# A hybrid decoder block on one core: thirteen Strassen pairs of V blocks instead of ten, their weights on SyncE's queue, and two groups of transposes moved

## The chip, the cores and the metric

The kernel runs on one core of a Trainium2 chip. The metric is the device time of one execution in microseconds, as the median of several runs. Engines are named as the profile names them: PE is TensorE's matmul and PEld its weight load, DVE is VectorE, ACT is ScalarE, POOL is GpSimd, SP is SyncE, which here does nothing but issue DMAs.

## What is computed

A decoder layer over 256 tokens of width 1024, in float32: two attention branches merged by gates, then a product-key expert mixer (PEER), residuals, and a last RMS norm. The mixer is the part that counts. There are 128 x 128 experts, each with a row u and a row v of 1024. Each token picks 16 experts for each of 8 heads, and

```python
act = gelu(einsum('td,thkd->thk', xc, u))     # u = expert_u[idx]
w = g * act                                   # g: softmax over the 16 best scores
y = einsum('thk,thkd->td', w, expert_v[idx])
```

The kernel does this densely: it multiplies all 16384 experts' u with all tokens, applies the gelu, multiplies by a matrix of gates that is zero where an expert was not picked, and multiplies the result with all of v.

## The kernel before

Weights come as a list of `units` of 128 partitions by up to 1024 columns, in the order of use: projections, attention's up-projections, gates, branches, `w_out`, queries, 128 U blocks, 128 V blocks. `emit_dma` takes the next unit, gives it a `raw` tile (a ring of 4) and has SyncE load it. `emit_split` splits the next unit into `hi` (ScalarE, L138) and `lo` = raw - hi (VectorE, for some stages POOL, L142), each in a ring of 4 tiles; it sees to it that three units beyond it are on their way. `wget(i)` splits up to unit i + 2 and hands out unit i. A product of two float32 matrices is three matmuls: hi with hi, hi with lo, lo with hi. All engines run their own instructions in the order in which the program emits them, and wait for each other through semaphores.

**Early.** `chunk(c)` multiplies the normed input with chunk c of the input projection, 4 units of 12 matmuls; `between` holds functions called behind a unit. Chunk 0 gives the latents, normed by `latent_norm` during chunk 1 (queries); `quad_T` transposes them (6 PE transposes, L263) and splits them into `cTh`, `cTl` (L272, L273) for the up-projections. Chunk 2 gives the keys, chunk 3 the values. `qa_evac` applies the rotary tables on VectorE and POOL (L410 to L417); `qa_T(1, kaT)` transposes the keys (8 PE transposes, L501; two copies by ScalarE, L503). Attention's first scores (L576) read `kaT`.

**U blocks.** `u_block` (wide, L851 and L853) and at the end `u_narrow` (L836 to L838) multiply block j of u with all tokens, and ScalarE writes the gelu into `gm[:, j, :]`, a tile of 128 x 128 x 256. The gates of the first 128 tokens lie in DRAM (`gd`), scattered there by POOL; the second half of the gelu of the first `NS` = 124 blocks is kept in `gld`, since the second tokens' gates are in `gm` already.

**V blocks.** `reload(j)` loads block j's part of `gd` and `gld` into `rl`; `a_mult(j)` multiplies `gm[:, j]` by it (L1161); `a_split(j)` makes `ah` (ScalarE, L1166) and `al` (VectorE, L1167) out of it, ring of 6 tiles of 256 columns; `v_mm(j, t)` adds block j for 128 tokens t to 1024 columns of the result in PSUM (L1188, 6 matmuls of 512 columns for each t).

**Strassen pairs.** For j in `WJ` the blocks j and j + 1 are taken together as a 2 x 2 product, in Winograd's form with seven products for eight (`w_mm`, L1265): 21 matmuls in place of 24. `w_pieces(j)` is a generator that one iteration at a time loads both blocks once more by POOL's queue (L1208, into spent parts of `gm`), forms four sums of their halves (L1211) and splits them (L1214, L1217) into `wsum`. `z_sums` and `z_split` do the like for the activations (L1247 to L1250, L1166, L1167). Four of the products collect in PSUM tiles `wm` over all pairs; `w_out` adds them to the residual after the last pair. The order of the V stage is written out by hand in its loop:

```python
for j in range(P):
    side += [w_pieces(i) for i in WJ if j == i - 11]
    a_split(j + 1); a_mult(j + 2); reload(j + 4)
    if j + 2 in WJ:
        a_mult(j + 3); z_sums(j + 2)
    vv[j] = (*wget(U_V[j]), *av.pop(j))
    if j + 1 in WJ:
        a_split(j + 2); z_split(j + 1)
    for g in side: next(g, None)
    # w_mm(j - 1) behind a pair, else v_mm(j, t) for both t
```

Of the kernel before, what the change touches and what calls it, by code (L numbers as in the profile page):

```python
# [11 lines left out]
F32 = mybir.dt.float32  # L12
# [5 lines left out]
OP = mybir.AluOpType  # L18
# [16 lines left out]
NB = 2  # L35
NP = 10

WJ = range(18, 108 + 1, 10)

C_ID, C_FREQ, C_W = 0, 128, 176  # L40
B_ID, B_MASK, B_I16, B_IOTA, B_W = 0, 128, 384, 640, 1664
# [3 lines left out]
def block_kernel(ctx, tc, consts, constb, pos, x, g_mix, g_ffn, g_fin, w_in, g_q, w_qup, g_kv, w_kvup,  # L45
# [68 lines left out]
    raw, split = {}, {}  # L114
    state = {"dma": 0, "split": 0, "end": len(units)}

    def emit_dma():
        i = state["dma"]
        if i >= state["end"]:
            return  # L120
        ap, w = units[i]
        raw[i] = wp.tile([P, 1024], F32, name="raw")
        nc.sync.dma_start(raw[i][:, :w], ap)
        state["dma"] += 1

    def emit_split(later=None, parts=1):
# [130 lines left out]
    def quad_T(src, dh, dl, t, b0, nb=4, scale=None, ps_=trt, diag=None, later=None):  # L257

        tr = ps_()
        for b in range(nb):  # L260
            bs = slice(b * P, (b + 1) * P)
            if diag is None:
                PE.transpose(tr[:, bs], src[:, bs], ident)  # L263
            else:
                PE.matmul(tr[:, bs], src[:, bs], diag, start=True, stop=True)
        tv = tr[:, :nb * P].rearrange("p (b n) -> p b n", b=nb)
        dst = (slice(None), slice(b0, b0 + nb), slice(t * P, (t + 1) * P))
        if later is not None:
            S.activation(dh[dst], tv, AF.Copy)
            later.append(lambda: V.tensor_tensor(dl[dst], tv, dh[dst].bitcast(F32), op=OP.subtract))  # L270
        elif scale is None:
            S.activation(dh[dst], tv, AF.Copy)  # L272
            V.tensor_tensor(dl[dst], tv, dh[dst].bitcast(F32), op=OP.subtract)  # L273
        else:
            S.activation(dh[dst], tv, AF.Copy, scale=scale)
            V.scalar_tensor_tensor(dl[dst], tv, scale, dh[dst].bitcast(F32), op0=OP.mult, op1=OP.subtract)
# [227 lines left out]

    qps = chunk(1, (lambda: latent_norm(0), lambda: latent_norm(1)))
    qa_evac(qps, 0)
    for t in range(NT):
        quad_T(cn[t][:, 512:], cTh, cTl, t, 0, nb=3)
    kps = chunk(2, (token_numbers,))
    qa_evac(kps, 1)  # L510
    qa_T(0, qaT)

# [19 lines left out]
    for hf in range(2):  # L532
        for t in range(NT):
# [7 lines left out]
            V.tensor_copy(vb[t][:, hf * 256:(hf + 1) * 256].rearrange("p (h z) -> p h z", h=4), kv[:, :, 64:])  # L541
            if hf == 0:
                G.tensor_copy(kd[:, :, 64:], kpe[:, t:t + 1, :].to_broadcast([P, H, 32]))
    vps = chunk(3)
    qa_T(1, kaT)
    for t in range(NT):
        S.activation(va[t], vps[t], AF.Copy, scale=rs1[t])

# [267 lines left out]
    def gelu_in(j, so, keep=False):  # L816
        S.activation(gm[:, j, T0], so[:, T0], AF.Gelu)
        if keep:
            gl = vpool[0].tile([P, T], F32, name="gl", tag="rl", bufs=4)[:, :P]
# [22 lines left out]
    def u_narrow(j, keep=False):  # L842
        gelu_in(j, u_mm(j), keep)
# [302 lines left out]
    av, rl = {}, {}  # L1146
    gview = gd.rearrange("(j i t) o -> j i (t o)", j=P, i=P)

    def reload(j):
        if j < P:  # L1150
            rl[j] = vp.tile([P, T], F32, name="rl", tag="rl", bufs=4)
            i = nc.sync.dma_start(rl[j][:, T0], gview[j]).ins
            for m in ends:
                tc.add_manual_dep(i, m.name, SYNC, reason="gates of all heads")
            if j < NS:
                nc.sync.dma_start(rl[j][:, T1], gld[j])

    def a_mult(j):
        if j in rl:
            w = T if j < NS else P  # L1160
            V.tensor_tensor(gm[:, j, :w], gm[:, j, :w], rl.pop(j)[:, :w], op=OP.mult)  # L1161

    def split2(src, w=T, **kw):
        h = vp.tile([P, T], F32R, name="ah", **kw)
        l = vp.tile([P, T], F32R, name="al", **kw)
        S.activation(h[:, :w], src, AF.Copy)  # L1166
        V.tensor_tensor(l[:, :w], src, h[:, :w].bitcast(F32), op=OP.subtract)  # L1167
        return h, l

    def a_split(j):  # L1170
        if j < P and j not in av:
            w = P if j in WJ else T
            av[j] = split2(gm[:, j, :w], w, tag="s1", bufs=6)

    yo = [[acc(), acc()], [acc(), acc()]]

# [17 lines left out]
    def spent(k):  # L1194
        return gm[:, 4 * k:4 * k + 4, :].rearrange("p a b -> p (a b)")

    copies = [[gm[:, 10 * k + a:10 * k + a + 4, :].rearrange("p a b -> p (a b)") for a in (0, 4)] for k in range(2)]
    zs = gm[:, 8:10, :].rearrange("p a b -> p (a b)")
    wsum = [h2[:, 2 * k:2 * k + 2].rearrange("p a z n -> p (a z n)") for k in range(4)]
    wm = {}  # L1200
    C0, C1 = slice(0, 512), slice(512, 1024)

    def w_pieces(j):
        r0, r1 = copies[WJ.index(j) % 2]

        def load(c):
            for k, r in enumerate((r0, r1)):
                G.dma_start(r[:, c], exp_v[:, j + k, c])  # L1208

        def add(o, a, b):  # L1210
            V.tensor_tensor(o, a, b, op=OP.add)  # L1211

        def upper(k):
            S.activation(wsum[2 * k], (r0, r1)[k], AF.Copy)  # L1214

        def lower(k, c):
            V.tensor_tensor(wsum[2 * k + 1][:, c], (r0, r1)[k][:, c], wsum[2 * k][:, c].bitcast(F32), op=OP.subtract)  # L1217

        load(C1)
        yield  # L1220
        load(C0)
        yield
        yield
        add(r1[:, C1], r1[:, C1], r0[:, C1])
        yield
        add(r0[:, C1], r0[:, C1], r0[:, C0])
        yield
        add(r0[:, C0], r0[:, C0], r1[:, C1])
        yield
        add(r1[:, C0], r1[:, C0], r0[:, C0])  # L1230
        yield
        upper(0)
        lower(0, C1)
        yield
        lower(0, C0)
        yield
        upper(1)
        lower(1, C0)
        yield
        lower(1, C1)  # L1240

    zz = {}

    def z_sums(j):
        a11, a21, a12, a22 = gm[:, j, T0], gm[:, j, T1], gm[:, j + 1, T0], gm[:, j + 1, T1]
        z = [zs[:, P * k:P * k + P] for k in range(4)]
        V.tensor_tensor(z[0], a22, a21, op=OP.subtract)  # L1247
        V.tensor_tensor(z[1], z[0], a11, op=OP.add)
        V.tensor_tensor(z[2], a11, a21, op=OP.subtract)
        V.tensor_tensor(z[3], a12, z[1], op=OP.subtract)  # L1250

    def z_split(j):
        zz[j] = [split2(zs[:, T * k:T * k + T], tag="z", bufs=4) for k in (1, 0)]

    def w_mm(j):
        (h0, l0, ah0, al0), (h1, l1, ah1, al1) = vv.pop(j), vv.pop(j + 1)
        z34, z12 = zz.pop(j)
        if not wm:
            for k, f in enumerate((trt, trt, sct, sct)):
                wm[k] = f()  # L1260

        def mul(o, st, ts, mv, cs, own=True):
            n = 0
            for a, b in ((0, 0), (0, 1), (1, 0)):
                PE.matmul(o, st[a][:, ts], mv[b][:, cs], start=own and j == WJ[0] and n == 0,  # L1265
                          stop=own and j == WJ[-1] and n == 2)
                n += 1

        s0, s1 = wsum[:2], wsum[2:]
        mul(wm[0], (ah0, al0), T0, (h0, l0), C0)  # L1270
        mul(yo[0][0], (ah1, al1), T0, (h1, l1), C0, False)
        mul(yo[0][1], z34, T1, (h1, l1), C1, False)
        mul(wm[1], z12, T0, s0, C1)
        mul(wm[2], z12, T1, s0, C0)
        mul(yo[1][0], (ah1, al1), T1, s1, C0, False)
        mul(wm[3], z34, T0, s1, C1)

    def w_out():

# [200 lines left out]
```

## Time and profile before

| | |
|---|---|
| median of 3 runs | 978.64 us (977.89 to 979.82) |
| the profiled execution | 974.74 us, of which the span is 973.0 |
| TensorE busy | 959.3 us, mean granted clock 0.997 |
| VectorE, ScalarE, POOL busy | 781.7, 605.7, 386.9 us |
| DMA | 217.51 MB, 224 GB/s over the span |
| U blocks | from about 245 to 623 us |
| V blocks | from 623 to 960 us |

A busy share is an average over stages, and TensorE's matmuls overlap, so its 99% does not say that it runs at its peak. What a stage is worth is read from what TensorE waits for in it, and from how far the other engines are from filling the time.

### The profile page before, as it was taken

How to read it: one execution, taken by the hardware profiler on the slowest of the kernel's cores; microseconds unless marked ns; L12 is line 12 of the kernel's file. 1: busy time of each engine (PE TensorE's matmuls, PEld its weight loads, DVE VectorE, ACT ScalarE, POOL GpSimd, SP SyncE). 2: the span in 40 equal slices, each digit the busy share in tenths (PEclk: the TensorE clock that was granted, in tenths of full speed). 3: DMA queues.
4: the chain of work that ended last, by engine and by line, in shares of the span. 5: the costliest groups of instructions: out<-in, count | busy, mean ns of one | idle time of the engine just before them, and what ended most of it. 6: DMA issues, size and time to landing. Idle time of an engine off the chain costs nothing.

```text
span 973.0 us, 16538 instructions
## 1 busy us (share of the span) xinstructions
PE 959.3 (99%) x5246; PEld 829.9 (85%) x5247; DVE 781.7 (80%) x1816; ACT 605.7 (62%) x1230; POOL 386.9 (40%) x289
## 2 busy tenths in 40 slices
PE   9999999999999999999999999999999999999996
PEld 6878888899998888888888888888888888888885
DVE  6845347658988888888888888689999999999984
ACT  6544453543566668888788877656666566656653
POOL 7644451177726877877877800001000000000001
PEclk9999999999999999999999999999999999999998
DMA  7755468564568888888988866798888988887871
GB/s 260 265 181 155 152 192 255 177 217 162 179 197 230 208 215 198 197 197 205 204 198 197 197 200 204 227 321 303 276 273 271 285 277 281 282 269 245 274 250 67
DMA packets 127945, 217.51 MB, mean 224 GB/s; under 512 B 29121, under 2 KB 78161, under 8 KB 127730
## 3 DMA queue, kind: packets, MB, share of 16 engines
q1 hardware_dynamic: 103248, 196.52, 64.1%
q0 software_dynamic: 20096, 11.25, 9.3%
q10 hardware_dynamic: 4514, 8.68, 2.3%
q8 instruction: 42, 0.69, 0.3%
q14 instruction: 45, 0.37, 0.1%
HBM read 197.72 MB, written 18.68 MB: 222 GB/s over the span
## 4 chain that ended last, share of the span: by engine, by line
PE 93%; POOL 2%; DMA 1%; DVE 1%; ACT 1%; issue 1%; SPq 0%; POOLq 0%; DVEq 0%; ACTq 0%
PE acc L1188 30%; PE tr L851 11%; PE sc L851 11%; PE tr L853 6%; PE sc L853 5%; PE sc L889 5%; PE acc L318 3%; PE acc L316 3%; PE acc L319 3%; PE acc L1265 2%; PE acc L1113 2%; PE sc L1265 1%; PE tr L1265 1%; PE sc L838 1%; PE sc L837 1%; PE sc L836 1%
## 5 line engine op out<-in xcount | busy, mean ns | idle before, releaser
L142 DVE TENSOR_TENSOR lo<-raw,hi 128x1024 fp32r<-128x1024 f32 (+1 forms) x277 | 332.2, 1202 | 53.0 <-ACT hi L138 51.0
L138 ACT ACTIVATE hi<-raw 128x1024 fp32r<-128x1024 f32 (+1 forms) x327 | 334.8, 1029 | 11.4 <-PE acc L319 5.2
L996 POOL DMA_INDIRECT gd<-gate,addr x128 | 210.8, 1647 | 78.9 <-issue 57.0
L1166 ACT ACTIVATE ah<-gm 128x256 fp32r<-128x256 f32 (+1 forms) x148 | 58.6, 409 | 131.9 <-DVE lo L142 71.4
L142 POOL TENSOR_TENSOR lo<-raw,hi 128x1024 fp32r<-128x1024 f32 x46 | 109.6, 2388 | 66.9 <-ACT hi L138 65.0
L1188 PE MATMUL acc<-hi,al 128*128 128x512 f32 x429 | 132.4, 389 | 0.0
L1188 PE MATMUL acc<-lo,ah 128*128 128x512 f32 x429 | 132.3, 389 | 0.0
L1188 PE MATMUL acc<-hi,ah 128*128 128x512 f32 x429 | 132.3, 389 | 0.0
L1208 POOL DMA_DIRECT2D gm<-in_exp_v_dram x40 | 21.8, 550 | 275.3 <-DVE h L1217 104.5
L851 PE MATMUL tr<-h,hi 128*128 128x512 f32 x464 | 116.2, 392 | 0.0
L851 PE MATMUL sc<-h,hi 128*128 128x512 f32 x448 | 112.3, 392 | 0.0
L851 PEld LDWEIGHTS tr<-h,hi 128*128 128x128 f32 x464 | 83.4, 189 | 14.9
L1188 PEld LDWEIGHTS acc<-hi,al 128*128 128x128 f32 x429 | 80.5, 188 | 16.8
L1188 PEld LDWEIGHTS acc<-lo,ah 128*128 128x128 f32 x429 | 80.5, 188 | 16.6
L1188 PEld LDWEIGHTS acc<-hi,ah 128*128 128x128 f32 x429 | 80.5, 188 | 16.6
L851 PEld LDWEIGHTS sc<-h,hi 128*128 128x128 f32 x448 | 80.6, 189 | 14.4
L1167 DVE TENSOR_TENSOR al<-gm,ah 128x256 fp32r<-128x256 f32 (+1 forms) x148 | 59.1, 410 | 14.6 <-ACT ah L1166 14.6
L853 PEld LDWEIGHTS tr<-h,lo 128*128 128x128 f32 x464 | 63.3, 190 | 4.5
L853 PEld LDWEIGHTS sc<-h,lo 128*128 128x128 f32 x448 | 61.1, 190 | 4.4
L853 PE MATMUL tr<-h,lo 128*128 128x256 f32 x464 | 64.7, 282 | 0.0
L853 PE MATMUL sc<-h,lo 128*128 128x256 f32 x448 | 62.5, 282 | 0.0
L1161 DVE TENSOR_TENSOR gm<-gm,rl 128x256 f32<-128x256 f32 (+1 forms) x128 | 52.1, 414 | 3.8 <-DMA rl<-gld 3.8
(343 smaller groups left out, 1668.3 us busy)
## 6 DMA issues: line engine op xcount, KB each, us to landing
raw<-in_exp_u_dram SPq DMA_DIRECT2D x128, 512.0 KB, 4.0
raw<-in_exp_v_dram SPq DMA_DIRECT2D x118, 512.0 KB, 4.8
raw<-in_w_in_dram SPq DMA_DIRECT2D x28, 512.0 KB, 3.5
gm<-in_exp_v_dram POOLq DMA_DIRECT2D x40, 256.0 KB
gd<-zero ACTq DMA_DIRECT2D x8, 1024.0 KB
raw<-in_w_pq_dram SPq DMA_DIRECT2D x16, 512.0 KB, 4.6
rl<-gd SPq DMA_DIRECT2D x128, 64.0 KB, 4.5
gld<-gs SPq DMA_DIRECT2D x124, 64.0 KB, 3.3
```

Of the source, the lines that this page charges most:

```text
L138: S.activation(hi[:, ks], r[:, ks], AF.Copy)
L142: e.tensor_tensor(lo[:, :w], r[:, :w], hi[:, :w].bitcast(F32), op=OP.subtract)
L316: PE.matmul(o, th[:, db, sl], lo[:, ws], start=False, stop=db == nd - 1)
L851: PE.matmul(s, hi[:, b * P:(b + 1) * P], h2[:, b].rearrange("p z n -> p (z n)"), start=b == 0, stop=False)
L853: PE.matmul(s[:, :T], lo[:, b * P:(b + 1) * P], h2h[:, b, :], start=False, stop=b == ND - 1)
L889: PE.matmul(q[:, :T], w[:, b * P:(b + 1) * P], m[:, b, :], start=k == 0 and b == 0, stop=k == 2 and b == ND - 1)
L996: i = nc.gpsimd.indirect_dma_start(out=gd[:, :], out_offset=bass.IndirectOffsetOnAxis(ap=addr[g][:, c], axis=0), in_=gate[g][:, c], in_off ...
L1161: V.tensor_tensor(gm[:, j, :w], gm[:, j, :w], rl.pop(j)[:, :w], op=OP.mult)
L1166: S.activation(h[:, :w], src, AF.Copy)
L1167: V.tensor_tensor(l[:, :w], src, h[:, :w].bitcast(F32), op=OP.subtract)
L1188: PE.matmul(o, st[:, sl], mv[:, c:d], start=j == (0 if own is None else P - LAST) and mv is hi and st is ah, stop=j == last and st is al)
L1265: PE.matmul(o, st[a][:, ts], mv[b][:, cs], start=own and j == WJ[0] and n == 0, stop=own and j == WJ[-1] and n == 2)
```

## The change

`WJ` becomes `range(18, 115, 8)`: 13 pairs, 8 blocks apart, where there were 10 at a distance of 10. The pieces of a pair are loaded by SyncE in place of POOL, once, into two fixed tiles `r0`, `r1`, from which the split of the two blocks is made as well (`loaded`); the sums go to tiles `xs` of their own and are split in four halves of 512 columns. `reload`, `a_mult` and `a_split` work on two blocks at a time. The z's are made by three operations in place of four and split into the unused columns of the first block's own `hi` and `lo`. In the early part, the transposes of the latents go behind the first unit of chunk 2 (the token numbers behind the second), and those of the keys behind the second unit of chunk 3.

```diff
-WJ = range(18, 108 + 1, 10)
+WJ = range(18, 114 + 1, 8)
...
         ap, w = units[i]
-        raw[i] = wp.tile([P, 1024], F32, name="raw")
-        nc.sync.dma_start(raw[i][:, :w], ap)
+        if i in loaded:
+            raw[i] = loaded.pop(i)
+        else:
+            raw[i] = wp.tile([P, 1024], F32, name="raw")
+            nc.sync.dma_start(raw[i][:, :w], ap)
...
-    for t in range(NT):
-        quad_T(cn[t][:, 512:], cTh, cTl, t, 0, nb=3)
-    kps = chunk(2, (token_numbers,))
+    def latent_T():
+        for t in range(NT):
+            quad_T(cn[t][:, 512:], cTh, cTl, t, 0, nb=3)
+    kps = chunk(2, (latent_T, token_numbers))
...
-    vps = chunk(3)
-    qa_T(1, kaT)
+    vps = chunk(3, (lambda: None, lambda: qa_T(1, kaT)))
...
     def reload(j):
         if j < P:
-            rl[j] = vp.tile([P, T], F32, name="rl", tag="rl", bufs=4)
-            i = nc.sync.dma_start(rl[j][:, T0], gview[j]).ins
+            rl[j] = vp.tile([P, 2, T], F32, name="rl", tag="rl", bufs=3)
+            i = nc.sync.dma_start(rl[j][:, :, T0], gview[j:j + 2].rearrange("j i t -> i j t")).ins
...
-            V.tensor_tensor(gm[:, j, :w], gm[:, j, :w], rl.pop(j)[:, :w], op=OP.mult)
+            V.tensor_tensor(gm[:, j:j + 2, :w], gm[:, j:j + 2, :w], rl.pop(j)[:, :, :w], op=OP.mult)
...
+            h, l = [vp.tile([P, 2 * T], F32R, name=n, tag="s1", bufs=4) for n in ("ah", "al")]
+            split2(gm[:, j:j + 2, :].rearrange("p a b -> p (a b)"), h, l)
...
+    r0, r1 = spent(0), spent(1)
+    xs = [gm[:, 8 + 2 * k:10 + 2 * k, :].rearrange("p a b -> p (a b)") for k in range(4)]
+    zs = gm[:, 16:18, :].rearrange("p a b -> p (a b)")
...
             for k, r in enumerate((r0, r1)):
-                G.dma_start(r[:, c], exp_v[:, j + k, c])
+                nc.sync.dma_start(r[:, c], exp_v[:, j + k, c])
+                loaded[U_V[j + k]] = r
...
         load(C1)
         yield
         load(C0)
         yield
         yield
+        add(2, r1[:, C1], r0[:, C1])
+        yield
+        add(0, r0[:, C1], r0[:, C0])
+        upper(2)
+        yield
+        add(1, r0[:, C0], xs[2])
+        lower(2)
+        upper(0)
+        yield
+        add(3, r1[:, C0], xs[1])
+        yield
+        lower(0)
+        upper(1)
+        yield
+        lower(1)
+        upper(3)
+        yield
+        lower(3)
...
     def z_split(j):
-        zz[j] = [split2(zs[:, T * k:T * k + T], tag="z", bufs=4) for k in (1, 0)]
+        zz[j] = [t[:, C1] for t in split[U_V[j]]]
+        split2(zs, *zz[j])
...
-        mul(wm[1], z12, T0, s0, C1)
-        mul(wm[2], z12, T1, s0, C0)
-        mul(yo[1][0], (ah1, al1), T1, s1, C0, False)
-        mul(wm[3], z34, T0, s1, C1)
+        mul(wm[1], z12, T0, s0, C0)
+        mul(wm[3], z34, T0, s1, C0)
+        mul(wm[2], z12, T1, s0, C1)
+        mul(yo[1][0], (ah1, al1), T1, s1, C1, False)
...
     reload(0)
-    reload(1)
     for j in range(done[0], P):
-        if j == P - 3:
+        if j == P - 2:
             a_mult(0)
-            a_mult(1)
             a_split(0)
         if j == P - 1:
             reload(2)
         u_narrow(j, True)
+    a_mult(2)
+    reload(4)
+    reload(6)
     side = []
-    reload(3)
     for j in range(P):
-        side += [w_pieces(i) for i in WJ if j == i - 11]
+        side += [w_pieces(i) for i in WJ if j == i - 8]
         if j == WJ[-1] + 2:
             side.append(w_out())
-        a_split(j + 1)
-        a_mult(j + 2)
-        reload(j + 4)
+        if j % 2:
+            a_split(j + 1)
+            a_mult(j + 3)
+            reload(j + 7)
         if j + 2 in WJ:
-            a_mult(j + 3)
             z_sums(j + 2)
         vv[j] = (*wget(U_V[j]), *av.pop(j))
         if j + 1 in WJ:
-            a_split(j + 2)
             z_split(j + 1)
```

More of the change, by code (lines that the diff above doesn't have):

```diff
@@ L113, in block_kernel @@
     lo_eng.update({U_U[j]: True for j in range(NP)})
-    raw, split = {}, {}
+    raw, split, loaded = {}, {}, {}
     state = {"dma": 0, "split": 0, "end": len(units)}
@@ L818, in gelu_in @@
         if keep:
-            gl = vpool[0].tile([P, T], F32, name="gl", tag="rl", bufs=4)[:, :P]
+            gl = vpool[0].tile([P, 2, T], F32, name="gl", tag="rl", bufs=3)[:, 0, :P]
         else:
@@ L1155, in reload @@
             if j < NS:
-                nc.sync.dma_start(rl[j][:, T1], gld[j])
+                nc.sync.dma_start(rl[j][:, :, T1], gld[j:j + 2].rearrange("j i t -> i j t"))
     def a_mult(j):
@@ L1160, in a_mult, with split2 @@
             w = T if j < NS else P
[L1161 to L1168, printed above, removed]
-    def a_split(j):
-        if j < P and j not in av:
-            w = P if j in WJ else T
-            av[j] = split2(gm[:, j, :w], w, tag="s1", bufs=6)
+            V.tensor_tensor(gm[:, j:j + 2, :w], gm[:, j:j + 2, :w], rl.pop(j)[:, :, :w], op=OP.mult)
+    def split2(src, h, l):
+        S.activation(h, src, AF.Copy)
+        V.tensor_tensor(l, src, h.bitcast(F32), op=OP.subtract)
+    def a_split(j):
+        if j < P:
+            h, l = [vp.tile([P, 2 * T], F32R, name=n, tag="s1", bufs=4) for n in ("ah", "al")]
+            split2(gm[:, j:j + 2, :].rearrange("p a b -> p (a b)"), h, l)
+            for k in range(2):
+                av[j + k] = h[:, k * T:k * T + T], l[:, k * T:k * T + T]
     yo = [[acc(), acc()], [acc(), acc()]]
@@ L1195, in spent @@
         return gm[:, 4 * k:4 * k + 4, :].rearrange("p a b -> p (a b)")
-    copies = [[gm[:, 10 * k + a:10 * k + a + 4, :].rearrange("p a b -> p (a b)") for a in (0, 4)] for k in range(2)]
-    zs = gm[:, 8:10, :].rearrange("p a b -> p (a b)")
+    r0, r1 = spent(0), spent(1)
+    xs = [gm[:, 8 + 2 * k:10 + 2 * k, :].rearrange("p a b -> p (a b)") for k in range(4)]
+    zs = gm[:, 16:18, :].rearrange("p a b -> p (a b)")
     wsum = [h2[:, 2 * k:2 * k + 2].rearrange("p a z n -> p (a z n)") for k in range(4)]
@@ L1203, in w_pieces, with add, half, lower @@
     def w_pieces(j):
-        r0, r1 = copies[WJ.index(j) % 2]
         def load(c):
             for k, r in enumerate((r0, r1)):
-                G.dma_start(r[:, c], exp_v[:, j + k, c])
-        def add(o, a, b):
-            V.tensor_tensor(o, a, b, op=OP.add)
+                nc.sync.dma_start(r[:, c], exp_v[:, j + k, c])
+                loaded[U_V[j + k]] = r
+        def add(k, a, b):
+            V.tensor_tensor(xs[k], a, b, op=OP.add)
+        def half(k):
+            return wsum[2 * (k // 2)][:, 512 * (k % 2):512 * (k % 2) + 512], \
+                wsum[2 * (k // 2) + 1][:, 512 * (k % 2):512 * (k % 2) + 512]
         def upper(k):
-            S.activation(wsum[2 * k], (r0, r1)[k], AF.Copy)
-        def lower(k, c):
-            V.tensor_tensor(wsum[2 * k + 1][:, c], (r0, r1)[k][:, c], wsum[2 * k][:, c].bitcast(F32), op=OP.subtract)
+            S.activation(half(k)[0], xs[k], AF.Copy)
+        def lower(k):
+            h, l = half(k)
+            V.tensor_tensor(l, xs[k], h.bitcast(F32), op=OP.subtract)
         load(C1)
@@ L1223, in w_pieces @@
         yield
-        add(r1[:, C1], r1[:, C1], r0[:, C1])
+        add(2, r1[:, C1], r0[:, C1])
         yield
-        add(r0[:, C1], r0[:, C1], r0[:, C0])
+        add(0, r0[:, C1], r0[:, C0])
+        upper(2)
         yield
-        add(r0[:, C0], r0[:, C0], r1[:, C1])
+        add(1, r0[:, C0], xs[2])
+        lower(2)
+        upper(0)
         yield
-        add(r1[:, C0], r1[:, C0], r0[:, C0])
+        add(3, r1[:, C0], xs[1])
         yield
-        upper(0)
-        lower(0, C1)
+        lower(0)
+        upper(1)
         yield
-        lower(0, C0)
+        lower(1)
+        upper(3)
         yield
[L1237 to L1240, printed above, removed]
+        lower(3)
     zz = {}
     def z_sums(j):
[L1245 to L1250, printed above, removed]
+        a = gm[:, j:j + 2, :].rearrange("p a (b n) -> p (a b) n", b=2)
+        z = zs.rearrange("p (b n) -> p b n", b=4)
+        V.tensor_tensor(z[:, 0:4:2], a[:, 0:4:3], a[:, 1:2].to_broadcast([P, 2, P]), op=OP.subtract)
+        V.tensor_tensor(z[:, 3], z[:, 2], a[:, 0], op=OP.add)
+        V.tensor_tensor(z[:, 1], a[:, 2], z[:, 3], op=OP.subtract)
     def z_split(j):
-        zz[j] = [split2(zs[:, T * k:T * k + T], tag="z", bufs=4) for k in (1, 0)]
+        zz[j] = [t[:, C1] for t in split[U_V[j]]]
+        split2(zs, *zz[j])
     def w_mm(j):
         (h0, l0, ah0, al0), (h1, l1, ah1, al1) = vv.pop(j), vv.pop(j + 1)
-        z34, z12 = zz.pop(j)
+        z = zz.pop(j)
+        z34, z12 = [[t[:, T * k:T * k + T] for t in z] for k in range(2)]
         if not wm:
```

## The prediction

> **What bounds the kernel now.** I read the page's head first, then the chain that ended last, then the stage that holds the V blocks by windows and as a timeline of VectorE, and last the two places ahead of it that the change touches.
>
> ```profile
> span 973.0 us, 16538 instructions
> PE 959.3 (99%) x5246; PEld 829.9 (85%) x5247; DVE 781.7 (80%) x1816; ACT 605.7 (62%) x1230; POOL 386.9 (40%) x289
> 623.32 48.99 PE acc L1188 x216
> 699.50 1.36 PE acc L1265 x6
> 703.59 21.76 PE acc L1188 x96
> 726.02 1.36 PE acc L1265 x6
> core 0: us, PE busy (x) PEld busy (x) DVE busy (x) ACT busy (x) POOL busy (x), PEclk, DMA share, GB/s
> 699.50:726.00 26.50, 26.50 (x119) 21.95 (x118) 24.52 (x45) 16.35 (x25) 2.15 (x5) 1.00 0.88 279
> ```
>
> The chain of work stays on TensorE through the V stage. 216 matmuls in 48.99 us are 0.2268 us each; between two Strassen pairs lie 726.02 - 699.50 = 26.52 us, and 8 x 12 + 21 = 117 matmuls at that pace are 26.53. So TensorE waits for nothing here, at a granted clock of 1.00, and a matmul taken away is worth 0.2267 us as long as the others keep up. VectorE is close behind: 24.52 of 26.50 us, 93%. That is the number the change must be held against.
>
> **The matmuls.** An ordinary pair of V blocks takes 24 matmuls, a Strassen pair 21. Ten pairs become thirteen: 3 x 3 x 0.2267 = 2.04 us less. The four products written in another order have the same count and width.
>
> **VectorE in the new period.** A pair now comes every 8 blocks: 6 x 12 + 21 = 93 matmuls, 21.08 us. What VectorE must do in that time is worked out from its spacing when nothing holds it:
>
> ```profile
> 698.16 1.22 DVE L142 TENSOR_TENSOR lo<-raw,hi 128x1024 fp32r<-128x1024 f32 x1
> 699.30 0.42 DVE L1167 TENSOR_TENSOR al<-gm,ah 128x256 fp32r<-128x256 f32 x1
> 699.63 0.41 DVE L1161 TENSOR_TENSOR gm<-gm,rl 128x256 f32<-128x256 f32 x1
> 708.58 0.68 DVE L1211 TENSOR_TENSOR gm<-gm 128x512 f32<-128x512 f32 x1
> 709.18 0.42 DVE L1167 TENSOR_TENSOR al<-gm,ah 128x256 fp32r<-128x256 f32 x1
> 718.46 0.29 DVE L1247 TENSOR_TENSOR gm<-gm 128x128 f32<-128x128 f32 x1
> 718.79 0.29 DVE L1248 TENSOR_TENSOR gm<-gm 128x128 f32<-128x128 f32 x1
> 719.00 0.28 DVE L1249 TENSOR_TENSOR gm<-gm 128x128 f32<-128x128 f32 x1
> 706.34 1.06 ACT L138 ACTIVATE hi<-raw 128x1024 fp32r<-128x1024 f32 x1
> 709.06 1.06 ACT L138 ACTIVATE hi<-raw 128x1024 fp32r<-128x1024 f32 x1
> 710.16 1.23 DVE L142 TENSOR_TENSOR lo<-raw,hi 128x1024 fp32r<-128x1024 f32 x1 [0.22 <-ACT hi L138]
> ```
>
> From start to start: 1024 columns 1.14 us, 512 columns 0.60, 256 columns 0.33, 128 columns 0.21, and 0.04 beyond its own duration where an operation reads the one before it (L1248 after L1247: 0.33). One operation's last 0.08 us lie under the next one. The gate products and the lower parts of the activations, two of 256 columns before, become one of 512 (0.60 for 0.67). The new period then holds 7 lower halves of V (7 x 1.14) and one of 512 (0.60), 4 gate products, 4 lower parts of activations, 4 sums and 4 lower parts of sums (16 x 0.60), three z sums (0.42 + 0.04, 0.29 + 0.04, 0.20) and one lower part of z (0.60): 19.8 us of 21.08, 94%. The same reckoning gives 23.8 for a period of before, where the window shows 24.52; the rest are the uncovered 0.08 of some eight operations with a wait behind them. So VectorE gets tighter by a point or two and still fits on average.
>
> It must fit in order, too. Count from the start of a pair's 21 matmuls. The z halves now sit in the unused columns of the first V block's own hi and lo, so that hi tile is free after matmul 17 (3.85 us) where it was free after matmul 3 (0.68). ScalarE starts the hi of the block four further when TensorE lets go (706.34, when the block begun at 703.59 with 12 matmuls ends at 706.31) and VectorE follows 1.10 us after that (709.06 to 710.16): it starts at 5.0. From there it has 19.8 us without a pause, and the last piece of it, the lower part of the fourth sum, ends at 24.85. It is needed by matmul 20 of the next pair, at 21.08 + 19 x 0.2267 = 25.39. I followed the other inputs through the eight steps with the same durations: the nearest is an activation's hi that ScalarE finishes at 10.4 and VectorE reaches at 10.8. A margin of 0.5 us in 20 remains, so I take no stall. The ends are nothing (TensorE waits for nothing here today, so there is no gain to find) and 12 periods times what the work lies above my count.
>
> **The loads of the pairs.** Before, POOL loads both blocks of a pair (four pieces) and SyncE loads them again for the split; after, SyncE loads once and the split reads these copies.
>
> ```profile
> raw<-in_exp_v_dram SPq DMA_DIRECT2D x118, 512.0 KB, 4.8
> gm<-in_exp_v_dram POOLq DMA_DIRECT2D x40, 256.0 KB
> 699.41 0.33 SPq L123 DMA_DIRECT2D raw<-in_exp_v_dram  x1
> 699.78 0.44 SPq L1152 DMA_DIRECT2D rl<-gd  x1
> ```
>
> Per period SyncE brings 6 x 512 KB, 4 x 256 KB and 8 x 128 KB of gates: 5.24 MB in 21.08 us, 249 GB/s where the window shows 279. Its issues per period: 6 blocks, 4 pieces and 8 gate loads of two heads' width, 18 where 8 blocks took 24 before, at 0.33 to 0.44 us each. In its queue each piece waits for the splits of the former pair, which end 2.2 us before that pair's matmuls start; the block behind it waits for a later split anyway. The pieces are first read 8.5 us after that start, and a block takes 4.8 us to land. Hidden, with over 3 us to spare; if that cover failed, one late microsecond would cost 13.
>
> **Keys.** Their eight transposes go from behind the chunk of values to behind its second unit.
>
> ```profile
> 46.78 0.73 POOL L417 TENSOR_TENSOR qk<-rc,rs 128x256 f32<-128x256 f32 x1
> 56.58 1.06 ACT L138 ACTIVATE hi<-raw 128x1024 fp32r<-128x1024 f32 x1 [1.66 <-PE acc L319]
> 62.74 1.04 PE L501 MATMUL tr<-ident,qk 128*128 128x128 f32 x8
> 63.38 1.08 ACT L503 ACTIVATE kaT<-tr 128x512 f32<-128x512 f32 x2 [5.73 <-PE tr L501]
> 64.51 0.70 PE L576 MATMUL sc<-kaT,qaT 64*128 64x256 f32 x2 [0.74 <-ACT kaT L503]
> 57.72 2.39 POOL L142 TENSOR_TENSOR lo<-raw,hi 128x1024 fp32r<-128x1024 f32 x1 [0.30 <-ACT hi L138]
> ```
>
> Now TensorE issues the transposes and then waits for ScalarE's copy: 0.74 us by the row, some 0.85 counted from the last transpose's issue. After, the rotated keys are there (POOL ends at 47.5, the second unit at about 57.5), ScalarE has a gap of 5.73 us for the copies, and the first scores follow the chunk at once: 0.8 us less. What queues behind the copies is two hi splits, later by up to 5 us, and POOL's two lower halves (2.39 each), done at about 62.6 and 65.0; the first is used at about 66.7. Late next is ScalarE's copy of the values, 0.65 us each, of which the first gate chunk's second accumulator needs one, at 65.8; it is done by 64.6.
>
> **Latents.** Six transposes and one wait go behind the first unit of the next chunk.
>
> ```profile
> 30.66 0.33 PE L263 MATMUL tr<-ident,cn 128*128 128x128 f32 x1 [0.26 <-DVE cn L481]
> 30.76 2.37 DVE L142 TENSOR_TENSOR lo<-raw,hi 128x1024 fp32r<-128x1024 f32 x2
> 32.68 1.07 PE L316 MATMUL acc<-lo,hTh 128*128 128x512 f32 x4
> ```
>
> The 0.26 us wait goes. But the unit moves up to 29.6, reaches its lower half at 31.4, and VectorE, held by the same latents, ends that at 30.76 + 1.22 = 31.98: a wait of 0.5 in its place. Four matmuls and 0.65 us of transposes behind it end at 33.6, where the unit ended before at 33.58. I take zero, between -0.3 and +0.3. The token numbers move one unit too; they change places with one lower half on VectorE, and nothing there is late.
>
> **From U to V.** Reloads come in pairs, and the first gate product and split stand one block later.
>
> ```profile
> 614.82 0.84 SPq L1156 DMA_DIRECT2D rl<-gld  x1
> 617.28 0.43 DVE L1161 TENSOR_TENSOR gm<-gm,rl 128x256 f32<-128x256 f32 x1 [2.09 <-DMA rl<-gld]
> 618.06 1.04 ACT L138 ACTIVATE hi<-raw 128x1024 fp32r<-128x1024 f32 x1
> 619.14 1.23 DVE L142 TENSOR_TENSOR lo<-raw,hi 128x1024 fp32r<-128x1024 f32 x1 [0.22 <-ACT hi L138]
> 619.81 0.28 PE L837 MATMUL sc<-h,hi 128*128 128x256 f32 x1
> 620.42 0.39 PE L838 MATMUL sc<-h,lo 128*128 128x256 f32 x1 [0.33 <-DVE lo L142]
> ```
>
> Today VectorE waits 2.09 us for the first gates with the last U block's split queued behind it, and TensorE, which issues every 0.12 us here, comes at 620.42 where it was due at 619.93: 0.49 us. After, that split stands ahead of the wait. What stands behind it is the first V block's split, which would end at about 621.3 and is needed from 622.7. The larger reloads may land half a microsecond later than 617.2; the 1.4 us hold that. 0.45 us less, between 0 and 0.5.
>
> **Sum.** -2.04 - 0.8 - 0 - 0.45 = -3.3 us. The profiled execution took 974.74 (973.0 of span and 1.7 around it) and would take 971.4; the median of the runs shown is 978.64, 3.9 above it, so 975.3 on that scale.
>
> **The rivals.** *VectorE sets the pace (slower).* The place is the last lower part of the sums, the price 1.2 us for each 0.1 us that the period's work lies above 19.8 + 0.5 = 20.3; from 20.6 on the gain of 3.3 us is spent. At 5% more than I counted, 20.8, it is 12 x 0.5 - 3.3 = +2.7: 981.3. For it: no stretch of 20 us without a pause on VectorE stands in the trace of before. Against: every duration is a row of this stage. Chance 0.08.
>
> *Operations that don't overlap at all.* With full durations the period is 7 x 1.22 + 18 x 0.68 + 1.0 = 21.8, past 20.3 by 1.5: 12 x 1.5 - 3.3 = +14.7, 993. But 699.30 follows a 1.22 us operation begun at 698.16 by 1.14, and a period of before with full durations, 9 x 1.22 + 21 x 0.42 + 9 x 0.68 + 5 x 0.29, would be 27.4, longer than the 26.52 it took. Chance 0.01. The Trainium skill, page "VectorE: DVE Perf Modes", section "The DRAIN you can't avoid", says that the next operation does not start until the pipe has emptied; by that rule this rival would be the forecast, and the trace disagrees by 0.08 us for each operation.
>
> *SyncE's queue gets late (slower).* A piece that waits holds the blocks behind it; 0.4 us per pair would be 13 x 0.4 - 3.3 = +1.9, 980.5. Against: 3 us of cover and fewer bytes. Chance 0.06.
>
> *The moved steps bring nothing.* The 0.8 and 0.45 us are taken up by a later wait (attention's ScalarE chain, the first V splits) and only the matmuls count: 978.64 - 2.04 = 976.6. For it: the latents show how a wait moves on. Chance 0.15.
>
> *No change.* New waits of a few tenths per pair eat what was won: 978.6. Chance 0.07.
>
> **The numbers.** The likeliest, 0.63, gives 975.3, its own range 974.4 to 976.2. About 0.2% (2 us) is what a measurement here can tell from no change: runs shown spread by 977.89 to 979.82. Faster by more than that: the 0.63 and two thirds of 0.15, 0.73. Same: the rest of that, the 0.07, and a part of the slower cases that end near zero, 0.17. Slower: 0.10. The range takes in the matmuls-only case, no change, and the runs' spread below: 973.8 to 978.8.
>
> **What would show it.** Right: pairs 21.1 us apart in the chain, no wait of TensorE for VectorE or DMA in the V stage, VectorE about 94% busy there, DMA near 250 GB/s; scores begin with the chunk's end, without a wait for ScalarE; no gap at the last U block; about 0.5 us of wait for a lower half in the chunk of keys. Wrong: waits of TensorE at the pair's last product, pairs further apart than 21.1, ScalarE waiting for blocks or pieces.

## The result, and the profile after

The changed kernel takes 975.02 us (median of 6 runs, 973.25 to 975.84) against 979.86 us of the kernel before in the same comparison: ratio 0.9949, interval 0.9937 to 0.996. That is 4.8 us, or 0.5%, faster. In a second comparison both kernels were 5 us quicker, and the same changed kernel took 969.90 against 974.89 us: ratio 0.9951 (0.9938 to 0.9965), 5.0 us. The forecast was 975.3 us, but as a gain it was 3.3 us. The time was met and the gain was not: some 1.6 us more were won than the sum holds.

The page's head of the kernel after:

```profile
span 973.1 us, 16001 instructions
PE 959.5 (99%) x5237; PEld 830.1 (85%) x5238; DVE 785.6 (81%) x1704; ACT 598.2 (61%) x1191; POOL 368.0 (38%) x249
```

Its chain of work, at the pairs' second products:

```profile
676.32 1.36 PE acc L1281 x6
697.40 1.36 PE acc L1281 x6
718.48 1.36 PE acc L1281 x6
```

Its window over one period (length, then busy us of PE, PEld, DVE, ACT and POOL with counts, granted clock, DMA share, GB/s):

```profile
676.30:697.40 21.10, 21.10 (x95) 17.48 (x94) 20.00 (x29) 12.77 (x18) 0.00 (x0) 1.00 0.79 248
```

The V stage is as forecast: the pairs stand 697.40 - 676.32 = 21.08 us apart, TensorE is busy in all of it, VectorE for 20.00 of 21.10 us (95%), and DMA moves 248 GB/s. The view of waits lists none of TensorE's in this stage.

The span of this execution, 973.1, cannot be held against the 973.0 of before. Around 310 us its engines stand still once, in a stage that the change does not touch (the view of waits of that stretch: total, times, longest):

```profile
PE tr L857 <- issue: 1.6, 1, 1.6
ACT us L864 <- remote: 9.7, 2, 7.8
DVE us L865 <- issue: 5.4, 2, 5.1
```

These waits stand in no other profile of this study. The wide U blocks, from the first to the last product of L857, took 338.1 us here and 333.0 in all the others. The 5.1 us of difference are about what the kernel after was slower by in the first comparison; whether its other executions there, and those of the kernel before, had such a pause too is not shown. So the stretches are measured in a second profile of the same kernel, called "again", whose span is 968.1 us. The rows that mark its stretches are the starts of the first scores, of the first V matmul and of the last one:

```profile
63.39 0.70 PE L582 MATMUL sc<-kaT,qaT 64*128 64x256 f32 x2
621.47 0.63 PE L1194 MATMUL acc<-hi,ah 128*128 128x512 f32 x2
960.81 0.28 PE L1194 MATMUL sc<-hi,al 128*128 128x256 f32 x1
```

In the kernel before the same marks are at 64.51, 623.2 and 964.5. That gives:

| stretch | before | again | difference | forecast |
|---|---|---|---|---|
| start to first scores | 64.5 | 63.4 | -1.1 | -0.8 |
| first scores to first V matmul | 558.6 | 558.1 | -0.6 | -0.45 |
| V stage, first to last matmul | 341.4 | 339.3 | -2.0 | -2.04 |
| last V matmul to the end of the span | 8.4 | 7.2 | -1.2 | 0 |
| span | 973.0 | 968.1 | -4.9 | -3.3 |

Three rows agree with the forecast within 0.3 us. The first of them is one execution against one, and this stretch differs between executions of the same code, as the last experiments show. The fourth difference, at the end, is not in the forecast.

### The profile page after: what moved, and what is told of

Same layout as the page of the kernel before. It is cut to its first block, busy times and chain, and to the rows that moved or that the text cites. A ratio compares the mean times of both kernels' runs of the same rounds, so it can differ in the third digit from the quotient of the medians.

```text
span 973.1 us, 16001 instructions
## 1 busy us (share of the span) xinstructions
PE 959.5 (99%) x5237; PEld 830.1 (85%) x5238; DVE 785.6 (81%) x1704; ACT 598.2 (61%) x1191; POOL 368.0 (38%) x249
## 4 chain that ended last, share of the span: by engine, by line
PE 95%; POOL 1%; issue 1%; DVE 1%; DMA 1%; ACT 0%; SPq 0%; another core or an unknown queue 0%; POOLq 0%; DVEq 0%
PE acc L1194 28%; PE tr L857 11%; PE sc L857 11%; PE tr L859 6%; PE sc L859 6%; PE sc L895 5%; PE acc L322 4%; PE acc L320 4%; PE acc L323 4%; PE acc L1281 3%; PE sc L1281 2%; PE tr L1281 2%; PE acc L1119 2%; PE sc L843 1%; PE sc L842 1%; PE sc L844 1%
## 5 line engine op out<-in xcount | busy, mean ns | idle before, releaser
L142 ACT ACTIVATE hi<-raw 128x1024 fp32r<-128x1024 f32 (+1 forms) x301 | 311.0, 1039 | 59.1 <-issue 22.1
L146 DVE TENSOR_TENSOR lo<-raw,hi 128x1024 fp32r<-128x1024 f32 (+2 forms) x251 | 306.2, 1223 | 50.6 <-ACT hi L142 47.7
L146 POOL TENSOR_TENSOR lo<-raw,hi 128x1024 fp32r<-128x1024 f32 x46 | 109.5, 2386 | 66.2 <-ACT hi L142 64.2
L1194 PE MATMUL acc<-lo,ah 128*128 128x512 f32 x405 | 125.0, 389 | 0.0
L1194 PE MATMUL acc<-hi,al 128*128 128x512 f32 x405 | 124.9, 389 | 0.0
L1194 PE MATMUL acc<-hi,ah 128*128 128x512 f32 x405 | 124.9, 389 | 0.0
L857 PE MATMUL tr<-h,hi 128*128 128x512 f32 x464 | 117.6, 396 | 1.6 <-issue 1.6
L857 PE MATMUL sc<-h,hi 128*128 128x512 f32 x448 | 112.3, 392 | 0.0
L857 PEld LDWEIGHTS tr<-h,hi 128*128 128x128 f32 x464 | 84.4, 191 | 16.9 <-issue 1.7
L857 PEld LDWEIGHTS sc<-h,hi 128*128 128x128 f32 x448 | 80.6, 189 | 14.4
L1194 PEld LDWEIGHTS acc<-hi,al 128*128 128x128 f32 x405 | 76.0, 188 | 15.8
L1194 PEld LDWEIGHTS acc<-lo,ah 128*128 128x128 f32 x405 | 76.0, 188 | 15.8
L1171 ACT ACTIVATE ah<-gm 128x512 fp32r<-128x512 f32 x64 | 40.5, 633 | 70.0 <-PE acc L1194 41.3
L859 PE MATMUL sc<-h,lo 128*128 128x256 f32 x448 | 62.8, 282 | 1.4 <-remote 1.1
L1172 DVE TENSOR_TENSOR al<-gm,ah 128x512 fp32r<-128x512 f32 x64 | 44.2, 690 | 11.7 <-ACT ah L1171 11.4
L864 ACT ACTIVATE us<-tr 128x256 f32<-128x256 f32 x58 | 22.2, 382 | 43.2 <-PE tr L859 34.2
```

The costliest lines, as they stand in the source:

```text
L142: S.activation(hi[:, ks], r[:, ks], AF.Copy)
L146: e.tensor_tensor(lo[:, :w], r[:, :w], hi[:, :w].bitcast(F32), op=OP.subtract)
L857: PE.matmul(s, hi[:, b * P:(b + 1) * P], h2[:, b].rearrange("p z n -> p (z n)"), start=b == 0, stop=False)
L859: PE.matmul(s[:, :T], lo[:, b * P:(b + 1) * P], h2h[:, b, :], start=False, stop=b == ND - 1)
L1171: S.activation(h, src, AF.Copy)
L1172: V.tensor_tensor(l, src, h.bitcast(F32), op=OP.subtract)
```

## The experiments

**The same kernel again, and the three parts one by one.** Four kernels ran in one comparison with the kernel before (974.89 us). The first is the kernel after, unchanged.

> The changed kernel once more, for a second profile and more runs. Theory one, three terms: stage by stage the two profiles differ by 2.03 us in the V blocks (337.09 to 335.06), 0.59 between U and V and 0.76 at the keys, 3.4 us in all, and what the medians showed beyond that (4.8 us) is spread from execution to execution; then it is 3.4 us faster than before, ratio 0.9965. Theory two, something more: 1.4 us come from a place not in the sum, such as the end (from the last VectorE operation to the end of the span 5.2 us before, 4.0 after) or POOL's queue; then again 4.8 us, ratio 0.995, and the 4.0 us at the end return in this profile.

Measured: 969.90 us, ratio 0.9951 (0.9938 to 0.9965). The second theory stands: 5.0 us is more than the three terms give.

The second puts the keys' transposes back.

```diff
-    vps = chunk(3, (lambda: None, lambda: qa_T(1, kaT)))
+    vps = chunk(3)
+    qa_T(1, kaT)
```

> The changed kernel with the transposes of the keys behind the whole chunk of values, as before. If their place is worth what the wait was: 0.8 us slower than the changed kernel, and the first scores wait 0.74 us for ScalarE again. If a later wait takes the gain up: no difference, and the profile shows the same start of the queries' stage as the changed kernel.

Measured: 971.12 us, ratio 0.9962 (0.9948 to 0.9975), 1.2 us slower than the kernel after. TensorE's wait is back in the view of waits (total, times, longest):

```profile
PE sc L583 <- ACT kaT L507: 0.7, 1, 0.7
```

The five runs of this kernel fall into two groups, 970.2 to 970.4 and 971.1 to 971.3 us. So the 1.2 us of the medians need not be the price of this wait alone.

The third has ten pairs, 8 blocks apart.

```diff
-WJ = range(18, 114 + 1, 8)
+WJ = range(18, 90 + 1, 8)
```

> The changed kernel with its first ten pairs only (18 to 90, still 8 apart). If TensorE sets the pace, 9 matmuls more at 0.2267 us: 2.0 us slower than the changed kernel, V stage 337.1 us. If VectorE had begun to hold the 8-block period, the three pairs left out give back more than they cost, and it is less than 2.0 slower or even.

Measured: 972.47 us, ratio 0.9976 (0.9967 to 0.9985), 2.6 us slower than the kernel after. Its V stage takes 341.4 us, as before the change: the three further pairs are worth 2.0 us there, and nine matmuls were priced at 2.04. In its profile the first scores start at 64.2 us and not at 63.4, which covers the rest.

The fourth hands the pairs' pieces back to GpSimd's queue.

```diff
-                nc.sync.dma_start(r[:, c], exp_v[:, j + k, c])
+                G.dma_start(r[:, c], exp_v[:, j + k, c])
```

> The changed kernel with the pairs' pieces loaded by POOL's queue in place of SyncE's (once, as in the changed kernel). Theory one: the queue doesn't matter, the same time as the changed kernel within 0.5 us, V stage 335.1 us. Theory two: the 1.4 us go back, 3.4 faster than before. Were SyncE's queue a burden, this would be the faster of the two.

Measured: 972.25 us, ratio 0.9973 (0.9964 to 0.9983), 2.3 us slower than the kernel after. Not one microsecond of that lies where the pieces are loaded and used: the V stage takes 339.3 us in both. It lies after the last V matmul, 9.4 us where the kernel after has 7.2, the stretch in which the unforecast 1.2 us stand. The next two kernels look for the cause.

**The end of the program.** The chain of work stops at VectorE's last operation, 5.1 us ahead of the end of the span in the kernel before, and the timeline shows only two stores after it. The view by source line has more. The program's last line (L1476 before, L1491 after) issues a DRAIN on each engine; the columns are count, shortest, median and longest in ns, and first and last start. Of the kernel before:

```profile
L1476 POOLq DRAIN  x3: 46/97/5732, 966.4 to 972.7; - x3
L1476 SPq DRAIN  x3: 7/7/7, 970.7 to 972.4; - x3
```

Of "again":

```profile
L1491 POOLq DRAIN  x3: 46/97/2464, 962.7 to 967.8; - x3
L1491 SPq DRAIN  x3: 7/7/7, 967.2 to 967.5; - x3
```

Of the kernel with GpSimd's loads:

```profile
L1491 POOLq DRAIN  x3: 46/97/6711, 962.1 to 969.4; - x3
L1491 SPq DRAIN  x3: 7/7/7, 966.4 to 969.1; - x3
```

The engines meet once before the program ends. SyncE comes there when the last store has landed: 970.7 us in the kernel before. GpSimd's DRAIN begins with its last operation at 966.4 and takes 5.73 us, to 972.2. So in the kernel before GpSimd comes last, by 1.5 us. In "again" its DRAIN takes 2.46 us, is over at 965.2, and SyncE comes last, at 967.2. In the kernel with GpSimd's loads it ends at 968.8, 2.4 us behind SyncE. With no, 40 and 52 pieces on GpSimd's queue the DRAIN takes 2.46, 5.73 and 6.71 us: (5.73 - 2.46) / 40 = (6.71 - 2.46) / 52 = 0.082 us a piece. Two kernels test this.

First, the kernel before with nothing but the queue changed:

```diff
-                G.dma_start(r[:, c], exp_v[:, j + k, c])
+                nc.sync.dma_start(r[:, c], exp_v[:, j + k, c])
```

> The kernel before, with one word changed: the 40 pieces of weights of its ten pairs are issued by SyncE instead of GpSimd. Theory one (GpSimd's closing DRAIN, the line of the program's end in the trace, sets the end: it runs 5.73 us in the kernel before and 2.46 us in the kernel after, and in the kernel before it ends 1.4 us after SyncE's own last DRAIN): the V stage stays at 341.4 us, GpSimd's DRAIN falls to about 2.5 us, and the whole gains 1.4 us, ratio 0.9986. Theory two (the 1.4 us belong to the kernel with thirteen pairs, not to the queue): no change, ratio 1.000. The prediction on record had this step at nothing.

Measured: 973.62 us against 974.73, ratio 0.9988 (0.9979 to 0.9997). The V stage stays at 341.4 us, the end shrinks from 8.4 to 7.0, and the DRAIN is the short one:

```profile
L1476 POOLq DRAIN  x3: 46/97/2466, 966.3 to 971.1; - x3
```

Second, the kernel after with the last five pairs' 20 pieces on GpSimd's queue:

```diff
-                nc.sync.dma_start(r[:, c], exp_v[:, j + k, c])
+                (G if j >= WJ[-5] else nc.sync).dma_start(r[:, c], exp_v[:, j + k, c])
```

> The kernel after, with the 20 pieces of the last five pairs issued by GpSimd and the first 32 by SyncE. From 0 pieces 2.46 us, 40 pieces 5.73 us and 52 pieces 6.71 us the DRAIN grows by 0.082 us a piece. Theory one (length by the piece, and it counts only once it outlasts SyncE's wait for the last store, 4.6 us after it starts): the DRAIN takes 4.1 us, ends 0.5 us ahead of SyncE's, and the time is that of the kernel after, ratio 0.995, end after the last matmul 7.3 us. Theory two (every piece on this queue costs at the end, 2.1 us for 52): 0.8 us slower than the kernel after, ratio 0.996. Theory three (what counts is that late pieces are still being worked off): the DRAIN is as long as with all 52, 6.7 us, and the kernel 2.1 us slower than the kernel after, ratio 0.9973.

Measured: 970.03 us, ratio 0.9948 (0.9935 to 0.9962), the time of the kernel after, and 7.0 us from the last V matmul to the end.

```profile
L1491 POOLq DRAIN  x3: 46/97/4097, 963.3 to 968.1; - x3
L1491 SPq DRAIN  x3: 7/7/7, 967.6 to 967.9; - x3
```

2.46 + 20 x 0.082 = 4.10 us were expected and 4.097 are there. The DRAIN ends at 967.4, 0.2 us ahead of SyncE, and costs nothing. So theory one holds in both kernels: the DRAIN grows by the piece, early or late pieces alike, and counts only where it outlasts the last store. The Trainium skill, page "VectorE: DVE Perf Modes", section "The DRAIN you can't avoid", tells of DRAINs from the runtime's preamble and postamble, on all five engines, as a constant of about 12 ns. Whether the DRAINs of the program's last line are among them is not shown here. SyncE's take 7 ns; GpSimd's 2.46 to 6.71 us are no such constant.

**How much room VectorE has.** One and then two operations of 512 columns more a pair, a lower half computed twice:

```diff
         add(3, r1[:, C0], xs[1])
         yield
+        lower(2)          # second kernel only
         lower(0)
         upper(1)
         yield
+        lower(0)          # both kernels
         lower(1)
```

> The kernel after, with one more VectorE operation of 512 columns a pair (a lower half computed twice, same result). It takes 0.60 us of VectorE's time in a period of 21.08. Theory one (what the trace after shows: last lower half ready 0.67 us before the matmul that reads it, VectorE idle 1.0 us in the period): it fits, the period stays 21.08 us and the time that of the kernel after, ratio 0.995. Theory two (the prediction's ledger, a margin of 0.5 us): PE waits 0.1 us a pair, 1.2 us in all, ratio 0.996.

> The kernel after, with two more VectorE operations of 512 columns a pair (two lower halves computed twice, same results): 1.2 us more in a period whose idle time is 1.0 us. Theory one (VectorE's sum sets the pace once it is full; all its idle time can be used): the period grows to 21.2 to 21.3 us, 1.5 to 2.5 us in all, ratio 0.9965 to 0.9975. Theory two (the deadline of the last lower half is what counts, 0.67 us of room): PE waits 0.53 us a pair, 6.4 us in all, ratio 1.0015. Theory three (VectorE is not near to setting the pace): no change, ratio 0.995.

Measured: 971.99 us, ratio 0.9969 (0.9958 to 0.998), 2.1 us slower than the kernel after, and 980.24 us, ratio 1.0053 (1.004 to 1.0067), 10.3 us slower. Both of my first theories fell. With one operation more the V stage takes 341.0 us, with two 349.3: 1.7 and 9.9 us more, 0.13 and 0.76 us for each of 13 pairs. One operation takes 0.60 us of VectorE, two 1.20; so 0.47 and 0.44 us of that fit in. This is close to the margin of 0.5 us in the prediction's ledger. Of the 0.67 us that the expectations read from the trace of after, not all is free; the rows of the kernel with two operations show why. From the timeline, VectorE's last lower half and TensorE's product that reads it:

```profile
718.72 0.69 DVE L1229 TENSOR_TENSOR h<-gm,h 128x512 fp32r<-128x512 f32 x1
719.46 0.50 PE L1283 MATMUL acc<-h,ah 128*128 128x512 f32 x1 [0.43 <-DVE h L1229]
```

And from the view of waits, over the whole stage:

```profile
PE acc L1283 <- DVE h L1229: 5.8, 13, 0.6
```

The half ends at 719.41, the product starts at 719.46 and takes 0.50 us where others take 0.39: 0.05 + 0.11 = 0.16 us go with the hand-over, and 0.67 - 0.16 = 0.51 us were free, near the 0.44 to 0.47 measured. VectorE's idle time is no measure of the room either. It is idle for 1.0 us in a period of the kernel after, and with two operations more, 1.2 us, TensorE waits 0.76 us a pair and not 0.2: a stop of some 0.45 us for a `hi` of ScalarE's stays in the period.

**Two sums on the idle engine.** The last kernel with its two operations too many, and two of the pair's four sums handed to GpSimd, which does nothing in this stage.

```diff
-            V.tensor_tensor(xs[k], a, b, op=OP.add)
+            (G if k in (0, 2) else V).tensor_tensor(xs[k], a, b, op=OP.add)
```

> The kernel of two more VectorE operations of 512 columns a pair (10.3 us slower than the kernel after), with two of the four sums a pair moved to GpSimd, which has no work in this stage: the same work for VectorE as in the kernel after, on another engine beside it. A sum of 512 columns takes GpSimd 1.30 us by the last rows of the kernel after. Theory one (VectorE's own sum with 0.5 us of margin sets it, and GpSimd's work lies beside it): the period is back at 21.08 us and the time at that of the kernel after, ratio 0.995. Theory two (GpSimd beside VectorE slows VectorE down, or its sums come late): a period of 21.3 us or more, 3 us slower than the kernel after or worse, ratio 0.998 and above.

Measured: 982.44 us, ratio 1.0077 (1.0063 to 1.0091): it should have come back by 10.3 us and got 2.2 slower. The two sums of one pair on GpSimd, one of its operations of this size at the kernel's end, and VectorE's two operations around the change from the first sum to the second:

```profile
694.66 5.62 POOL L1218 TENSOR_TENSOR gm<-gm 128x512 f32<-128x512 f32 x1 [14.66 <-DMA gm<-in_exp_v_dram]
700.24 1.74 POOL L1218 TENSOR_TENSOR gm<-gm 128x512 f32<-128x512 f32 x1
969.91 1.30 POOL L1370 TENSOR_TENSOR gm<-gm 128x512 f32<-128x512 f32 x1 [48.09 <-DVE gm L1366]
699.25 1.59 DVE L1172 TENSOR_TENSOR al<-gm,ah 128x512 fp32r<-128x512 f32 x1
700.76 1.78 DVE L1168 TENSOR_TENSOR gm<-gm,rl 128x512 f32<-128x512 f32 x1
```

The first sum takes GpSimd 5.62 us and the second 1.74, where the one at the kernel's end takes 1.30. Beside the first, VectorE works on without a gap until 699.12, each operation in its usual time. Then it pauses for 0.13 us, and its next two operations, begun while a sum is under way, take 1.59 and 1.78 us instead of 0.69. All pairs but the first look like this. VectorE is spared 1.2 us a pair and loses 0.90 + 1.09 = 2.0 us. Of the 0.8 us between them only 0.13 reach the period, 21.98 us for 21.85 with all sums on VectorE, mostly because its stop of 0.45 us for a `hi` is used up first. The sums do not come late: the view of waits lists no engine that waits for one. The Trainium skill says it (page "SBUF — State Buffer", section "Who interferes with whom"): a VectorE operation with two inputs in SBUF and a GpSimd operation that reads SBUF use one read interface, and the one that comes second is blocked. The trace agrees: both kinds of operation here read two tiles, GpSimd's first sum ends 1.2 us after VectorE's first pause, about the length of a sum with nothing beside it, and after that pause it is VectorE that is held up.

**The small moves.** The first gate product and split back where they were:

```diff
-        if j == P - 2:
+        if j == P - 3:
```

> The kernel after, with the first gate product and the first split of activations back at their old place, three U blocks from the end instead of two. Theory one (the prediction's: the split of the last U block queues on VectorE behind the wait for the first gates, and TensorE comes late): the stretch from the last U block to the first V block grows from 12.7 us by 0.5 to 0.6 us, ratio 0.9955 where the kernel after has 0.995; the gap ahead of the last U block's products is back. Theory two (the step is shorter because the gates come in pairs): no change.

Measured: 971.94 us, ratio 0.9968 (0.9957 to 0.9979), 2.0 us slower. The stretch from the last product of L857, in the last wide U block, to the first V matmul takes 14.1 us for 12.7. TensorE's waits there:

```profile
PE sc L842 <- ACT gl L828: 0.5, 1, 0.5
PE sc L844 <- DVE lo L146: 0.4, 1, 0.4
```

And VectorE's place in the timeline that holds them up:

```profile
617.22 0.69 DVE L1168 TENSOR_TENSOR gm<-gm,rl 128x512 f32<-128x512 f32 x1 [2.45 <-DMA rl<-gld]
```

Theory one is right in kind, but the stretch grew by 1.4 us and not by 0.5 to 0.6. From one start to the next TensorE's two stops take 0.63 and 0.59 us beyond its usual 0.12; that is 1.2 of the 1.4 us. The kernel before has one such stop, of 0.49 us, for the lower half. The other comes by way of ScalarE: its split behind the gate product waits 3.50 us for VectorE, and the copy `gl` that TensorE waits for stands behind that split. So the move is worth more than the 0.6 us by which the stretch got shorter. Gates that come in pairs keep VectorE waiting 2.45 us here, and 2.09 in the kernel before; whether that alone makes the second stop was not tried.

The latents' transposes back ahead of the chunk of keys:

```diff
-    kps = chunk(2, (latent_T, token_numbers))
+    latent_T()
+    kps = chunk(2, (token_numbers,))
```

> The kernel after, with the transposes of the latents back ahead of the chunk of keys. Theory one (the stretch behind it ends with the rotation of the keys on GpSimd and VectorE, not with TensorE): no change, 0.3 us at most either way, ratio 0.995. Theory two (part of the 0.3 to 0.4 us that the keys' move brought beyond its own row of 0.74 us is the latents'): 0.3 to 0.5 us slower, ratio 0.9955.

Measured: 970.14 us, ratio 0.9953 (0.9939 to 0.9966): 0.2 us from the kernel after, no difference that can be told.

And the keys' move alone, made in the kernel before:

> The kernel before, with the transposes of the keys alone moved behind the second unit of the chunk of values. Theory one (the prediction's 0.8 us, the row's wait of 0.74): 0.7 to 0.9 us faster than the kernel before, ratio 0.9992, and the scores begin without a wait. Theory two (the 1.2 us by which the kernel after got slower without this move): ratio 0.9988.

Measured: 974.16 us against 975.09, ratio 0.9991 (0.9982 to 1.0), 0.9 us, with an interval that reaches no change. With the 1.2 us of the kernel that undoes it, the move is worth about 1 us, and the runs do not tell the row's 0.74 us from 1.2. One reason lies ahead of the keys' transposes. In six of the ten profiles of kernels with the latents moved, TensorE waits for a lower half in the chunk of keys. The view of waits has it, here of the kernel with ten pairs:

```profile
PE acc L320 <- DVE lo L146: 0.3, 1, 0.3
```

From start to start it costs 0.34 to 0.51 us. The other four, "again" among them, do not have it. The first scores start at 63.8 to 64.2 us in the six. In the four they start at 62.8 to 63.4, or at 63.9 where the keys are put back. So a part of the 1.1 us in the table above comes from "again" being without this wait, which the prediction had reckoned with. What decides whether it comes is not shown.

## Why the prediction was right, and where it was not

- **The matmuls** (2.04 us). Right: the stage lost 2.0 us, and with ten pairs 2.0 us come back.
- **VectorE in the new period** (94%, a margin of 0.5 us, no stall). Right in its result: 95% measured, no wait of TensorE, and 0.44 to 0.47 us of further work fit in. One step on the way was wrong, "that hi tile is free after matmul 17", so that the next chain "starts at 5.0". Rows of the kernel after, from a pair whose matmuls start at 696.56:

```profile
698.80 1.07 ACT L142 ACTIVATE hi<-raw 128x1024 fp32r<-128x1024 f32 x1 [0.86 <-PE acc L1281]
699.52 0.69 DVE L1229 TENSOR_TENSOR h<-gm,h 128x512 fp32r<-128x512 f32 x1
700.13 1.22 DVE L146 TENSOR_TENSOR lo<-raw,hi 128x1024 fp32r<-128x1024 f32 x1
705.38 1.22 DVE L146 TENSOR_TENSOR lo<-raw,hi 128x1024 fp32r<-128x1024 f32 x1 [0.39 <-ACT hi L142]
```

ScalarE starts that `hi` 2.2 us after the pair, and VectorE the lower half at 3.6. It waits 0.86 us for a matmul of the pair, and the one that ends just ahead of it, at 698.76, is matmul 9, the last to read the second block. So this `hi` takes the tile of the pair's second block, not of the first. The chain without a pause starts later, at the stop for the next `hi`, 8.8 us after the pair. That the margin still came out at 0.5 is in part luck: the chain starts elsewhere and the length was right.

- **VectorE sets the pace** (rival, 0.08; "1.2 us for each 0.1 us" above the margin). It did not happen, and its price was right: two more operations put the work 0.7 us past the margin, 12 x 0.7 = 8.4 by its rule, and 9.9 were measured over 13 pairs.
- **Operations that don't overlap** (0.01). Excluded: a period with full durations would be 21.8 us, and 21.08 are there. The prediction quotes the Trainium skill, page "VectorE: DVE Perf Modes", section "The DRAIN you can't avoid", only in part: the section adds that a next operation that is not held starts earlier. So by the whole section this rival need not have been the forecast, and the overlap of 0.08 us does not contradict it.
- **SyncE's queue gets late** (0.06). It did not. The view of waits, over 625 to 960 us of the kernel after, has these for a transfer (total, times, longest):

```profile
ACT hi L142 <- DMA raw<-in_exp_v_dram: 3.1, 4, 1.1
DVE gm L1168 <- DMA rl<-gld: 0.9, 1, 0.9
```

ScalarE's four waits for a block end by 639 us, ahead of the first pair, none is for a piece, and TensorE waits behind none of them. (The gate loads in the prediction's count are of two blocks' width, not of two heads'; its bytes are right.)

- **Keys** (0.8 us). Right in its mechanism: the wait of 0.74 us is gone and the scores follow the chunk. In size about 1 us, which the runs do not tell from 0.8.
- **Latents** (0, but with "a wait of 0.5 in its place"). The zero was right as far as the runs can tell. The wait of 0.5 us for a lower half, named as a sign, comes in six of ten profiles, at 0.34 to 0.51 us. In the other four, the two of the kernel after among them, the lower half is there before the unit reaches it.
- **From U to V** (0.45 us, at most 0.5). 0.6 us, above its upper bound. Right in its mechanism, as the 1.4 us without the move show.
- **The loads of the pairs** ("Hidden"). This is the step that failed. It asked where the pieces are used and what lies behind them in SyncE's queue, and both were indeed free. It did not ask what 40 pieces on GpSimd's queue, long landed, still cost at the end. The row of 5732 ns and SyncE's 970.7 stand in the profile of before, but the prediction took the chain's last operation for the end. Term missing: 1.2 us by the stretches, 1.1 us by the kernel before with SyncE's loads.

With this term and the sizes measured in the two profiles the sum is -2.0 (V stage) - 1.1 (up to the first scores) - 0.6 (from there to the first V matmul) - 1.2 (the end) = -4.9 us. The forecast of 975.3 fell on 975.02 because the kernel before, in the comparison with it, took 979.86 us and not the 978.64 that the sum was made against; that shift of 1.2 us covered most of the 1.6 missing. So the time was met by luck.

## What to carry to other kernels

Look past the last operation of the chain: what the closing line of the program waits for on each engine is part of the time, and work that an engine's DMA queue did hundreds of microseconds earlier can be in it. A margin on an engine that is 95% busy is measured from the operation that is read first to its reader, hand-over included, and not by adding up idle time; and one surplus operation costs what lies beyond it, in every period. An engine that stands idle is not free room if the two slow each other when both read tiles, as GpSimd and VectorE did here.

## What the runs showed of the hardware that I had not expected

- GpSimd's closing DRAIN takes 2.46 us without pieces on its queue and 0.082 us more for each 256 KB piece, by four points (0, 20, 40, 52 pieces: 2.46, 4.10, 5.73, 6.71 us), whether the pieces came early or late. What the 2.46 us consist of was not tried; the 128 indirect transfers and four other loads of the same queue were in every kernel.
- GpSimd and VectorE, each working on two tiles in SBUF, slow each other: sums of 5.62 and 1.74 us for 1.30 on GpSimd, and 1.59 and 1.78 us for 0.69 on VectorE. GpSimd's first sum of a pair ended only after VectorE had paused.
- A lower half written by VectorE reaches the waiting product some 0.16 us after its row ends.
